# An encoder layer in three stages: its SBUF pools in another order, and two groups of loads on GpSimd's queue

## The chip, the cores and the metric

One core of one Trainium2 chip runs the whole kernel. The metric is the device time of one execution in microseconds (us). TensorE (PE) multiplies, VectorE (DVE), ScalarE (ACT) and GpSimd (POOL) do the rest, SyncE (SP) issues DMAs. Lines such as L42 or L1061 are lines of the kernel file.

## The reference

One encoder layer on a sequence of 2048 tokens of width 1024, all in float32:

```python
mod = silu(c) @ w_ada + b_ada                      # six vectors: shift, scale, gate, twice
h = rmsnorm(x, g_norm1) * (1 + sc1) + sh1
q_sb, k_sb, v_sb, q_ca, k_ca, v_ca = split(h @ w_in)     # 8 + 8 heads of 64
o_sb = stick_breaking_attention(q_sb, k_sb, v_sb)  # causal; weights from a running product
o_ca = chunked_relpos_attention(rms(q_ca), rms(k_ca), v_ca, rel_bias)  # own chunk + 8 before
x = x + gt1 * (concat(o_sb, o_ca) @ w_o)
h = rmsnorm(x, g_norm2) * (1 + sc2) + sh2
x = x + gt2 * (square(relu(h @ w1)) @ w2)          # 4096 wide in the middle
```

## The kernel before

Tokens are cut into four blocks of 512 (tb or g = 0 to 3, the latest first), width into eight slices of 128. A float32 product is made of three matmuls: each operand is split into a high part (ACT casts it, L128) and a low part (DVE or POOL subtracts, L129), and `mm3` multiplies high by high, high by low and low by high. What one stage hands to the next lies in DRAM scratch tensors: `scr_q`, `scr_k`, `scr_v`, `scr_w` (split weights), `scr_wo` (split w_o), `scr_m` (attention outputs), `scr_x` (the residual stream), `scr_h`, `scr_hid`, `scr_s`.

**Stage 1, projections.** Norm of x, the modulation vectors (`ada`), and the projections of most pieces of w_in. The last job is piece 5 for block 1. Tiles: `cb`, `cs` (pool adap), `wa` (adaw), `xt` (xp), the normed blocks `wide`, `ht2`, `ht0` (hp), the raw, high and low weights `wr`, `wh`, `wl` (wp), stores and turned heads (stp), norms (np_).

**Stage 2, attention.** A list of units (a head and a block of 512 queries, with 512 keys for the stick-breaking heads SB, or 1024 for the chunk heads CA), each of four steps. A step's order on PE, ACT, DVE and POOL is written out by hand (`Ordered` keeps each of these queues in the order of the program): transposes of weights made 8 steps ago (`wt`), scores of the next (`z`, `cz`), running product (`p`, a scan on DVE) or softmax, splits `wth`, `wtl`, value products (`acc`). POOL multiplies `b` by `p`, or scales `e`. Between the steps `fill` hands PE other matmuls as credit allows: the projections left over (`fill_qkv`: weights `fw`, banks `pf`) and the output projection of a finished block (`outproj(g)`, g = 3, 2, 1: weights `ow`, operand `mx`, banks `po`, residual `xr`). `outproj` loads `mo` (three buffers) and splits it slice by slice in `part(k)`; `part(k)` also starts the load of slice k + 3. What is left of the fillers runs after the last step (`drain`). Loads of q, k and v go through SP, those of the first two units through POOL's queue (`ldq`).

**Stage 3, MLP.** SP, ACT, DVE and POOL are not held to the order of the program here; the compiler's scheduler sets it from its own model, and PE keeps the program's. First the output projection of block 0: eight steps `Mixed(0, n)`, each 24 matmuls in one bank (`pso`). Step 0 loads the eight slices of `scr_m` (tile `m`, shown as `cm`) and splits them (`opm`); each step loads two halves of split weights (`wo`, four buffers) and a slice of x (`cxr`); `residual` (L209, DVE) adds, and SP stores to `scr_x` (L210). Then the first MLP product as seven sub-products of a Strassen-like scheme (`First`), whose right operands `h{i}_{k}` come from `right_blocks(mb, k)`, k = 0 to 3: four slices of `scr_x` loaded into temporaries `y` (pool tp, seven buffers, shown as `ty`), each multiplied by the row norm on POOL (L1062) and by scale and shift on ACT (L1063), then summed and split into seven `h` tiles. Then `Second`, the same for w2.

**Where tiles lie.** Pools of one stage are laid one behind the other in the order in which they are opened, and those of the next stage start again at the same place. The list `RESTS` sets how many steps a filler rests at each `yield` of a word ("pause" 3, "next" 1, "start" 10). In KB per partition, counted from the end of what lives through stages 1 and 2 (the 32 KB before that place, -32 to 0, hold pool hxp: the odd blocks `ht1`, `ht3`, later `mx`), worked out from the sizes of the tiles:

| stage | before |
|---|---|
| 1 | adap 0-8, adaw 8-24, xp 24-44, hp 44-76, wp 76-124, stp 124-156, np_ 156-167 |
| 2 | kp (q, k, v) 0-44, fp (`fw`/`ow`, `st`, `mo`, `xr`) 44-92, wtp (`wth`, `wtl`) 92-108, zp (`b`/`e`, `p`/`s`) 108-153, op (`o`, `otmp`, bias) 153-168 |
| 3 | hop (28 tiles `h`) -32-80, opp (split operands) 80-112, rawp (raw weights, `wo`) 112-128, accp (`cm`, `cxr`, kept sums) 128-152, tp 152-166, np2 from 166 |

Nothing in the source says what a tile waits for; the compiler derives the semaphores from which memory was used before.

Of the kernel before, what the change touches and what calls it, by code (L numbers as in the profile page):

```python
# [67 lines left out]
def encoder_kernel(ctx, tc, xT, c, g1, g2, w_in, gqk, bias, w_o, w1, w2, w_ada, b_ada, out):  # L68
# [151 lines left out]
    with ExitStack() as ph:  # L220
        adap = ph.enter_context(tc.tile_pool(name="adap", bufs=1))
        adaw = ph.enter_context(tc.tile_pool(name="adaw", bufs=4))
        xp = ph.enter_context(tc.tile_pool(name="xp", bufs=KT + 2))
        hp = ph.enter_context(tc.tile_pool(name="hp", bufs=1))
        wp = ph.enter_context(tc.tile_pool(name="wp", bufs=2))
        stp = ph.enter_context(tc.tile_pool(name="stp", bufs=4))
        np_ = ph.enter_context(tc.tile_pool(name="np_", bufs=2))
        pp = ph.enter_context(tc.tile_pool(name="ppA", bufs=8, space=PSUM))
# [298 lines left out]


    with ExitStack() as ph:
        kp = ph.enter_context(tc.tile_pool(name="kp", bufs=3))  # L530
        fp = ph.enter_context(tc.tile_pool(name="fp", bufs=3))
        wtp = ph.enter_context(tc.tile_pool(name="wtp", bufs=4))
        zp = ph.enter_context(tc.tile_pool(name="zp", bufs=2))
        op = ph.enter_context(tc.tile_pool(name="op", bufs=2))
        ppz = ph.enter_context(tc.tile_pool(name="ppz", bufs=4, space=PSUM))
        ppo = ph.enter_context(tc.tile_pool(name="ppo", bufs=2, space=PSUM))
# [226 lines left out]
        def fill_qkv(tb, ht, pieces):  # L763
# [12 lines left out]
            for n, piece in enumerate(pieces):  # L776
                grp, hf = divmod(piece, 2)
                w, nxt = nxt, []
                for j in range(2):
                    nm = f"f{tb}_{piece}_{j}"  # L780
                    ps = ppd.tile([P, TB], F32, tag="ps", name=f"p{nm}")
                    last = 0 if grp < 2 else 1
                    for tt in range(last + 1):
                        tl = slice((2 * j + tt) * P, (2 * j + tt + 1) * P)
                        for k in range(KT):
                            if n + 1 < len(pieces) and j and tt == last and k in (0, 4):
                                nxt.append(load(pieces[n + 1], k // 4))
                            wk = w[k // 4][:, k % 4]
                            for i, (a, b) in enumerate(((0, 0), (0, 1), (1, 0))):
                                flags = {"start": k == 0 and i == 0, "stop": k == KT - 1 and i == 2}  # L790
                                if grp < 2:
                                    pe.matmul(ps, wk[:, a, j * P : (j + 1) * P], ht[:, k, b, :], **flags)
                                    yield 1.0
                                else:
                                    pe.matmul(ps[:, tt * CW : (tt + 1) * CW], ht[:, k, b, tl], wk[:, a, :], **flags)
                                    yield 0.5

                    def keep():
                        if grp < 2:
                            store_qk(grp, 0, ps, fp, hf * 2 + j, tb, nm)  # L800
                        else:
                            store_v(grp // 3, ps, fp, hf, tb, j, nm)
                        if j:
                            have.add((piece, tb))

                    yield keep

        def outproj(g):
# [18 lines left out]
                fetch(k)  # L827
            nxt = load(0)
            yield "pause"
            part(0)  # L830
            yield "next"
            part(1)
            yield "next"
            for n in range(KT):
                w, xr = nxt
                if n + 1 < KT:
                    nxt = load(n + 1)
                ps = ppd.tile([P, TB], F32, tag="ps", name=f"po{g}_{n}")
                for k in range(KT):
                    if n == 0 and k + 2 < KT:  # L840
                        part(k + 2)
                    for i, (l, m) in enumerate(((0, 0), (0, 1), (1, 0))):
                        pe.matmul(
                            ps, w[:, l, k, :], mx[:, k, m, :], start=k == 0 and i == 0, stop=k == KT - 1 and i == 2
                        )
                        yield 1.0
# [154 lines left out]
    scr_hid = scratch("scr_hid", [P, 2, TB], 2, 8, NP // 2)  # L1001
    scr_s = scratch("scr_s", [P, 2, TB], 7, NP // 2)
    with ExitStack() as ph:
        hop = ph.enter_context(tc.tile_pool(name="hop", bufs=1))
        opp = ph.enter_context(tc.tile_pool(name="opp", bufs=8))
        rawp = ph.enter_context(tc.tile_pool(name="rawp", bufs=4))
        accp = ph.enter_context(tc.tile_pool(name="accp", bufs=12))
        tp = ph.enter_context(tc.tile_pool(name="tp", bufs=7))
        np2 = ph.enter_context(tc.tile_pool(name="np2", bufs=2))
        pp = ph.enter_context(tc.tile_pool(name="ppM", bufs=8, space=PSUM))  # L1010

# [45 lines left out]
        def right_blocks(mb, k):  # L1057
            y = {}
            for nm, tb, kk in (("11", 2 * mb + 1, k), ("12", 2 * mb, k), ("21", 2 * mb + 1, k + HK), ("22", 2 * mb, k + HK)):
                t = y[nm] = temp(f"y{mb}_{k}_{nm}")  # L1060
                sp.dma_start(t, scr_x[tb, kk])  # L1061
                pool.tensor_tensor(t, t, rows[tb], op=ALU.mult)  # L1062
                act.activation(t, t, AF.Identity, scale=aff[:, 1, kk : kk + 1], bias=mod[:, 3 * KT + kk : 3 * KT + kk + 1])  # L1063

            def put(i, src):
                hops[i, k] = hop.tile([P, 2, TB], F32R, tag=f"h{i}_{k}", name=f"h{mb}_{i}_{k}")
                operand(src, "", dst=hops[i, k])

# [187 lines left out]
        class Mixed(Step):  # L1256
# [9 lines left out]
            def prepare(self):  # L1266
                g, n = self.g, self.n
                if n == 0:
                    for k in range(KT):
                        m = kept(f"m{g}_{k}")  # L1270
                        sp.dma_start(m, scr_m[g, k])
                        Mixed.parts[k] = operand(m, f"m{g}_{k}", dve if k % 2 else pool)

            def load(self):
# [21 lines left out]

        steps += [Mixed(0, n) for n in range(KT)]
        for k in range(HK):
            at(2 + k, lambda k=k: right_blocks(1, k))
        for mb in (1, 0):  # L1300
            if mb:
                for j in range(NP):
# [64 lines left out]
```

## Time and profile before

| | us |
|---|---|
| median of 3 runs | 2782.63 (2777.75 to 2788.34) |
| the profiled execution | 2779.07 |
| its span, first to last instruction | 2777.3 |
| PE busy | 2644.2 (95%) |
| DVE, ACT, POOL busy | 1996.5, 1510.8, 1077.7 |
| stage 1, until the last projection matmul | about 494 |
| stage 2, until the last output projection matmul of its fillers | 494 to 1474 |
| stage 3 | 1474 to 2777 |

PE's busy time is the union of its matmuls, so its idle time is what the other 5% hold. In a row of the timeline stand start, duration, engine, line, operation, tile written and tiles read, how many instructions were merged, and in brackets the idle time of the engine before the row with what ended it. SPq and POOL rows of DMAs show the issue, not the transfer. The releaser in brackets is inferred from semaphores; where several were awaited, the last event stands there, and a DMA named there can be another one that shares its semaphore.

### The profile page before, as it was taken

Reading aid. Unit: us, or ns where it says so; the run is one execution under the profiler, and the core shown is the slowest. Engines: PE = TensorE matmul, PEld = TensorE weight load, DVE = VectorE, ACT = ScalarE, POOL = GpSimd, SP = SyncE. Lnnn points to the kernel's source line nnn. Section 1 sums busy time; section 2 is a strip of 40 time slices with the busy share of each in tenths; the row PEclk is TensorE's granted clock in tenths of the full one; section 3 lists DMA queues with packets and bytes.
Section 4 is the critical chain, followed back from the end, with each engine's and each line's share of the span. In section 5 each row is a group of like instructions: output and inputs, shape, how many; then the busy total and the mean of one; then the engine's idle time right before and its main releaser. Section 6 shows DMA issues by size and latency. Waiting matters only on the chain. (4 is left out here: it accounts for less than half of the span.)

```text
span 2777.3 us, 43035 instructions
## 1 busy us (share of the span) xinstructions
PE 2644.2 (95%) x14192; PEld 2244.7 (81%) x14192; DVE 1996.5 (72%) x3365; ACT 1510.8 (54%) x2884; POOL 1077.7 (39%) x1126
## 2 busy tenths in 40 slices
PE   5899989889999999989997999999999999999999
PEld 4699989678888997868786788888878888888887
DVE  8467576679789887979775887876587666655564
ACT  2322332678678878878763454455455445444443
POOL 5334364456546656777734433200021433300000
PEclk9899989899999999999998999999999999999999
DMA  7788975788887578655567777786567444465574
GB/s 249 252 302 291 347 244 207 237 243 244 268 262 234 193 210 261 195 169 185 169 206 263 252 275 260 268 291 239 188 243 266 152 148 167 152 208 191 196 257 171
DMA packets 309919, 635.71 MB, mean 229 GB/s; under 512 B 29248, under 2 KB 118336, under 8 KB 300608
## 3 DMA queue, kind: packets, MB, share of 16 engines
q1 hardware_dynamic: 309184, 631.39, 68.0%
q8 instruction: 112, 1.84, 0.3%
q0 software_dynamic: 512, 1.57, 0.2%
q14 instruction: 111, 0.91, 0.1%
HBM read 449.87 MB, written 182.98 MB: 228 GB/s over the span
## 5 line engine op out<-in xcount | busy, mean ns | idle before, releaser
L42 PE MATMUL ps<-oph,opv 128*128 128x512 f32 x2688 | 614.3, 390 | 3.7 <-DVE oph L129 2.0
L42 PE MATMUL ps<-h,opw 128*128 128x512 f32 x2688 | 610.2, 389 | 1.4 <-DVE cx L1019 1.1
L42 PEld LDWEIGHTS ps<-oph,opv 128*128 128x128 f32 x2688 | 505.1, 188 | 110.9 <-DVE oph L129 3.0
L42 PEld LDWEIGHTS ps<-h,opw 128*128 128x128 f32 x2688 | 504.3, 188 | 107.0 <-DVE cx L1019 1.5
L42 POOL TENSOR_TENSOR b<-b,p 128x512 f32<-128x512 f32 (+1 forms) x320 | 360.1, 1125 | 193.4 <-DVE p L42 174.3
L42 DVE TENSOR_TENSOR wtl<-wt,wth 128x512 fp32r<-128x512 f32 (+3 forms) x544 | 290.5, 545 | 50.4 <-ACT wth L42 47.5
L42 ACT CAST wth<-wt 128x512 fp32r<-128x512 f32 (+3 forms) x544 | 257.9, 484 | 117.0 <-PE wt L42 99.6
L42 PE MATMUL pt<-wh,ht 128*128 128x256 f32 x1664 | 311.1, 288 | 5.5 <-DVE ht L182 5.5
L129 DVE TENSOR_TENSOR oph<-hr,oph 128x512 fp32r<-128x512 f32 x224 | 155.6, 694 | 188.5 <-ACT oph L128 188.4
L128 ACT CAST oph<-hr 128x512 fp32r<-128x512 f32 x224 | 139.2, 622 | 276.1 <-PE ps L42 258.5
L42 PEld LDWEIGHTS pt<-wh,ht 128*128 128x128 f32 x1664 | 265.9, 195 | 6.8 <-DVE ht L182 6.7
L42 DVE TENSOR_TENSOR_SCAN p<-z,p,zero 128x512 f32<-128x512 f32 x192 | 245.9, 1281 | 35.2 <-ACT z L42 31.3
L42 PE MATMUL pt<-wl,ht 128*128 128x256 f32 x832 | 238.2, 286 | 0.0
L42 PE MATMUL acc<-wth,v 128*128 128x512 f32 (+3 forms) x544 | 221.7, 411 | 1.3 <-DMA v<-scr_v 1.3
L42 ACT ACTIVATE b<-z 128x512 f32<-128x512 f32 (+1 forms) x320 | 171.5, 536 | 68.0 <-PE z L42 40.6
L42 PE MATMUL z<-k,q 128*128 128x512 f32 (+3 forms) x640 | 188.9, 378 | 15.4 <-DVE p L42 11.4
L42 POOL TENSOR_TENSOR e<-e,cols 128x640 f32<-128x640 f32 (+4 forms) x128 | 143.5, 1123 | 147.9 <-DVE cols L42 110.9
L1019 POOL TENSOR_TENSOR ts<-w 128x512 f32<-128x512 f32 x32 | 45.3, 1415 | 363.8 <-DMA w<-in_w_dram 234.9
L42 PE MATMUL acc<-wtl,v 128*128 128x512 f32 (+3 forms) x544 | 186.2, 349 | 0.0
L42 PE MATMUL po<-mx,ow 128*128 128x512 f32 x576 | 164.9, 401 | 11.7 <-POOL mx L42 7.5
L42 PE MATMUL wt<-ident,b 128*128 128x128 f32 x1088 | 173.2, 275 | 1.8 <-DVE p L42 0.7
L42 ACT ACTIVATE z<-z 128x512 f32<-128x512 f32 (+1 forms) x320 | 170.1, 532 | 0.0
(211 smaller groups left out, 4760.3 us busy)
## 6 DMA issues: line engine op xcount, KB each, us to landing
hr<-scr_hid SPq DMA_DIRECT2D x112, 512.0 KB, 3.3
v<-scr_v SPq DMA_DIRECT2D x136, 256.0 KB, 3.7
k<-scr_k SPq DMA_DIRECT2D x268, 128.0 KB, 4.1
w<-in_w_dram SPq DMA_DIRECT2D x64, 512.0 KB, 4.1
wr<-scr_s SPq DMA_DIRECT2D x64, 512.0 KB, 4.2
q<-scr_q SPq DMA_DIRECT2D x124, 256.0 KB, 4.9
fw<-scr_w SPq DMA_DIRECT2D x28, 1024.0 KB, 7.0
wa<-in_w_ada_dram SPq DMA_DIRECT2D x48, 512.0 KB, 6.4
```

Of the source, the lines that this page charges most:

```text
L42: return lambda *x, **y: self.tc.keep_in_program_order(f(*x, **y))
L128: act.copy(hi, src)
L129: (lo_eng or dve).tensor_tensor(lo, src, hi.bitcast(F32), op=ALU.subtract)
L1019: eng.tensor_tensor(out, a, b, op=op)
```

## The change

Four things, none of which changes what is computed or how many instructions of a kind run:

- The pools are opened in another order, one (`st` of stage 2, now pool fsp) is taken out of fp, and hop is cut in three: hop1 holds the seven `h` tiles of k = 1 and one of k = 2, hop0 those of k = 0, hop2 the other thirteen.
- `outproj` does four `part`s at a step each before its first matmul, where it did two, and the last four between the first row's matmuls, where it did six.
- The eight loads of `m` and the sixteen loads of `y` for mb = 1 (blocks 3 and 2) are issued by POOL, where SP issued them.
- `right_blocks(1, k)` is called at steps 0, 2, 4, 6, where it was called at 2, 3, 4, 5.

| stage | after |
|---|---|
| 1 | adap 0-8, adaw 8-24, xp 24-44, wp 44-92, hp 92-124, stp 124-156, np_ 156-167 |
| 2 | zp 0-45, kp 45-89, fp 89-125, fsp 125-137, wtp 137-153, op 153-168 |
| 3 | hop1 -32-0, opp 0-32, rawp 32-48, accp 48-72, tp 72-86, hop2 86-138, hop0 138-166, np2 from 166 |

```diff
@@ -221,8 +221,8 @@
         adap = ph.enter_context(tc.tile_pool(name="adap", bufs=1))
         adaw = ph.enter_context(tc.tile_pool(name="adaw", bufs=4))
         xp = ph.enter_context(tc.tile_pool(name="xp", bufs=KT + 2))
+        wp = ph.enter_context(tc.tile_pool(name="wp", bufs=2))
         hp = ph.enter_context(tc.tile_pool(name="hp", bufs=1))
-        wp = ph.enter_context(tc.tile_pool(name="wp", bufs=2))
         stp = ph.enter_context(tc.tile_pool(name="stp", bufs=4))
         np_ = ph.enter_context(tc.tile_pool(name="np_", bufs=2))
         pp = ph.enter_context(tc.tile_pool(name="ppA", bufs=8, space=PSUM))
@@ -527,10 +527,11 @@
 
 
     with ExitStack() as ph:
+        zp = ph.enter_context(tc.tile_pool(name="zp", bufs=2))
         kp = ph.enter_context(tc.tile_pool(name="kp", bufs=3))
         fp = ph.enter_context(tc.tile_pool(name="fp", bufs=3))
+        fsp = ph.enter_context(tc.tile_pool(name="fsp", bufs=3))
         wtp = ph.enter_context(tc.tile_pool(name="wtp", bufs=4))
-        zp = ph.enter_context(tc.tile_pool(name="zp", bufs=2))
         op = ph.enter_context(tc.tile_pool(name="op", bufs=2))
         ppz = ph.enter_context(tc.tile_pool(name="ppz", bufs=4, space=PSUM))
         ppo = ph.enter_context(tc.tile_pool(name="ppo", bufs=2, space=PSUM))
@@ -797,9 +798,9 @@
 
                     def keep():
                         if grp < 2:
-                            store_qk(grp, 0, ps, fp, hf * 2 + j, tb, nm)
+                            store_qk(grp, 0, ps, fsp, hf * 2 + j, tb, nm)
                         else:
-                            store_v(grp // 3, ps, fp, hf, tb, j, nm)
+                            store_v(grp // 3, ps, fsp, hf, tb, j, nm)
                         if j:
                             have.add((piece, tb))
 
@@ -827,18 +828,17 @@
                 fetch(k)
             nxt = load(0)
             yield "pause"
-            part(0)
-            yield "next"
-            part(1)
-            yield "next"
+            for k in range(4):
+                part(k)
+                yield "next"
             for n in range(KT):
                 w, xr = nxt
                 if n + 1 < KT:
                     nxt = load(n + 1)
                 ps = ppd.tile([P, TB], F32, tag="ps", name=f"po{g}_{n}")
                 for k in range(KT):
-                    if n == 0 and k + 2 < KT:
-                        part(k + 2)
+                    if n == 0 and k + 4 < KT:
+                        part(k + 4)
                     for i, (l, m) in enumerate(((0, 0), (0, 1), (1, 0))):
                         pe.matmul(
                             ps, w[:, l, k, :], mx[:, k, m, :], start=k == 0 and i == 0, stop=k == KT - 1 and i == 2
@@ -1001,11 +1001,13 @@
     scr_hid = scratch("scr_hid", [P, 2, TB], 2, 8, NP // 2)
     scr_s = scratch("scr_s", [P, 2, TB], 7, NP // 2)
     with ExitStack() as ph:
-        hop = ph.enter_context(tc.tile_pool(name="hop", bufs=1))
+        hop1 = ph.enter_context(tc.tile_pool(name="hop1", bufs=1))
         opp = ph.enter_context(tc.tile_pool(name="opp", bufs=8))
         rawp = ph.enter_context(tc.tile_pool(name="rawp", bufs=4))
         accp = ph.enter_context(tc.tile_pool(name="accp", bufs=12))
         tp = ph.enter_context(tc.tile_pool(name="tp", bufs=7))
+        hop2 = ph.enter_context(tc.tile_pool(name="hop2", bufs=1))
+        hop0 = ph.enter_context(tc.tile_pool(name="hop0", bufs=1))
         np2 = ph.enter_context(tc.tile_pool(name="np2", bufs=2))
         pp = ph.enter_context(tc.tile_pool(name="ppM", bufs=8, space=PSUM))
 
@@ -1058,11 +1060,12 @@
             y = {}
             for nm, tb, kk in (("11", 2 * mb + 1, k), ("12", 2 * mb, k), ("21", 2 * mb + 1, k + HK), ("22", 2 * mb, k + HK)):
                 t = y[nm] = temp(f"y{mb}_{k}_{nm}")
-                sp.dma_start(t, scr_x[tb, kk])
+                (pool if mb else sp).dma_start(t, scr_x[tb, kk])
                 pool.tensor_tensor(t, t, rows[tb], op=ALU.mult)
                 act.activation(t, t, AF.Identity, scale=aff[:, 1, kk : kk + 1], bias=mod[:, 3 * KT + kk : 3 * KT + kk + 1])
 
             def put(i, src):
+                hop = hop0 if k == 0 else hop1 if k == 1 or (k, i) == (2, 1) else hop2
                 hops[i, k] = hop.tile([P, 2, TB], F32R, tag=f"h{i}_{k}", name=f"h{mb}_{i}_{k}")
                 operand(src, "", dst=hops[i, k])
 
@@ -1268,7 +1271,7 @@
                 if n == 0:
                     for k in range(KT):
                         m = kept(f"m{g}_{k}")
-                        sp.dma_start(m, scr_m[g, k])
+                        pool.dma_start(m, scr_m[g, k])
                         Mixed.parts[k] = operand(m, f"m{g}_{k}", dve if k % 2 else pool)
 
             def load(self):
@@ -1296,7 +1299,7 @@
 
         steps += [Mixed(0, n) for n in range(KT)]
         for k in range(HK):
-            at(2 + k, lambda k=k: right_blocks(1, k))
+            at(2 * k, lambda k=k: right_blocks(1, k))
         for mb in (1, 0):
             if mb:
                 for j in range(NP):
```

## The prediction

> **What bounds the kernel now.** I read the page, then PE's own list of waits, then the timeline of every engine where those waits lie.
>
> ```profile
> span 2777.3 us, 43035 instructions
> PE 2644.2 (95%) x14192; PEld 2244.7 (81%) x14192; DVE 1996.5 (72%) x3365; ACT 1510.8 (54%) x2884; POOL 1077.7 (39%) x1126
> PE z L42 <- DVE p L42: 11.4, 11, 6.6
> PE pso L42 <- DMA wo<-scr_wo: 7.7, 4, 4.8
> PE po L42 <- POOL mx L42: 7.5, 3, 5.1
> PE pso L42 <- DMA cxr<-in_xT_dram: 7.3, 1, 7.3
> PE po L42 <- ACT mx L42: 4.2, 1, 4.2
> ```
>
> PE is idle 2777.3 - 2644.2 = 133 us of the span. The rows of waits (total, times, longest) name what this change can reach: `pso`, 15 us, is the start of stage 3; `po`, 11.7 us, the output projections inside attention; the one wait of 6.6 us on `p` is the start of attention. No matmul is removed, so the change can give back only idle time, and the slow matmuls behind it.
>
> **From attention to the MLP (the main term).** PE's timeline, then one stretch of windows each for the waits and for steady running (PEclk, the granted clock, is third from the end):
>
> ```profile
> 1452.30 22.02 PE L42 MATMUL po<-mx,ow 128*128 128x512 f32 x96
> 1481.64 0.79 PE L42 MATMUL pso<-opm,wo 128*128 128x512 f32 x1 [7.32 <-DMA cxr<-in_xT_dram]
> 1501.86 14.02 PE L42 MATMUL pso<-opm,wo 128*128 128x512 f32 x48 [4.78 <-DMA wo<-scr_wo]
> 1517.00 5.75 PE L42 MATMUL pso<-opm,wo 128*128 128x512 f32 x24 [1.12 <-DMA wo<-scr_wo]
> 1541.30 3.35 PE L42 MATMUL ps<-h,opw 128*128 128x512 f32 x14
> 1502.00:1517.00 15.00, 13.88 (x48) 10.84 (x48) 12.26 (x18) 6.59 (x10) 6.58 (x3) 0.80 0.75 250
> 1517.00:1541.30 24.30, 22.39 (x95) 17.52 (x95) 18.47 (x26) 12.65 (x20) 10.71 (x7) 1.00 0.83 280
> ```
>
> From 1452.30 to 1474.32 PE does nothing but drain the fillers, 96 matmuls of 22.02 / 96 = 0.229 us. The 192 matmuls of `Mixed` then take from 1474.32 to 1541.30, 67.0 us, where 192 x 0.229 = 44.0 would do; behind the wait of 4.78 us the granted clock is 0.80 over 15 us, so a wait costs more than its length. Why the first waits:
>
> ```profile
> 1480.97 4.26 ACT L128 CAST opm<-cm 128x512 fp32r<-128x512 f32 x8 [27.89 <-DMA cxr<-in_xT_dram]
> 1475.14 0.32 SPq L210 DMA_DIRECT2D scr_x<-xr  x1
> scr_x<-xr SPq DMA_DIRECT2D x24, 256.0 KB, 4.6
> 1453.84 0.32 SPq L578 DMA_DIRECT2D scr_m<-o  x1
> DMA to landing us min/median/max: 6.8/6.8/6.8
> L42 POOL TENSOR_TENSOR mx<-mo,mx x8: 1277/1286/1297, 1361.0 to 1381.4; 128x512 fp32r<-128x512 f32 x8
> 1450.28 0.49 PE L42 MATMUL wt<-ident,e 128*128 128x128 f32 x3
> 1452.19 0.27 PE L42 MATMUL acc<-wtl,v 128*128 128x128 f32 x1
> ```
>
> The row of landings belongs to the one `scr_m` store above it.
>
> All eight casts start together at 1480.97, 5.8 us after the store of the last `xr` was issued. The first `opm` buffer lies on `mo`, not on `xr`, and `mo` was last read by the `mx` split that starts at 1381.4: the wait is for the pool fp as a whole. In the new layout opp lies on zp, whose last reader (a transpose of `e`) ends at 1450.8, rawp on zp and kp, accp and tp on kp, whose last reader (a value product) ends at 1452.5. So `cm`, four `wo`, `cxr` and seven `y` can be loaded and split under the 22 us of drain; only `cm`'s last slice waits for the store issued at 1453.84. It lands at 1460.7, so the load behind it has 13.6 us until 1474.3 and another 21 x 0.229 = 4.8 until slice 7 is used. The 24 loads are 24 x 0.62 us (below) = 15 us of POOL's time, and POOL is idle there. The two first rows of `Mixed` then run at 24 x 0.229 = 5.5 us; the other six reload `wo` behind the row two before, at the pace that rows 4 to 7 show now, (1541.30 - 1517.00) / 4 = 6.1. Sum 2 x 5.5 + 6 x 6.1 = 47.6, against 67.0: 19.4 us. I take 18, since the loads are now bunched beside the last `ow`. Bounds: 67.0 - 44.0 = 23.0 above, and 7.3 below (the first wait alone).
>
> What would be late next is `h`: `First` needs all four k.
>
> ```profile
> L129 DVE TENSOR_TENSOR h<-ty,h x28: 678/685/1786, 1494.8 to 1539.3; 128x512 fp32r<-128x512 f32 x28
> 1489.66 7.98 POOL L1062 TENSOR_TENSOR ty<-ty,r 128x512 f32<-128x512 f32 x6
> ```
>
> 28 tiles in 44.5 us now end 2 us before PE needs them, no slack. After: hop0 lies on wtp and op, free when the last `scr_m` store has landed (1460.7), so k = 0 goes under the drain; hop1 is hxp, free at 1474.3; hop2 holds fp and still waits until about 1481. Then three blocks remain, each 7 splits and 4 sums x 0.685 = 7.5 us of DVE: about 1504, before `Mixed` ends at 1522. The calls at 4 and 6 in place of 4 and 5 stay inside that.
>
> **From projections to attention.** The end of stage 1 on PE, SP and ACT, with POOL's present loads and the groups of DMAs (the last number is us from issue to landing):
>
> ```profile
> 494.26 1.04 PE L42 MATMUL px<-ident,qh 128*128 128x128 f32 x8
> 494.49 0.33 SPq L771 DMA_DIRECT2D fw<-scr_w  x1
> 504.45 0.60 ACT L42 ACTIVATE b<-z 128x512 f32<-128x512 f32 x1 [8.24 <-DMA scr_k<-st]
> 506.85 1.22 PE L42 MATMUL z<-k,q 128*128 128x512 f32 x2 [6.64 <-DVE p L42]
> 396.12 1.24 POOL L545 DMA_DIRECT2D q<-scr_q  x2 [5.47 <-issue]
> q<-scr_q POOLq DMA_DIRECT2D x4, 256.0 KB, 12.4
> 510.21 1.08 SPq L545 DMA_DIRECT2D q<-scr_q  x2
> q<-scr_q SPq DMA_DIRECT2D x124, 256.0 KB, 4.9
> fw<-scr_w SPq DMA_DIRECT2D x28, 1024.0 KB, 7.0
> 516.25 1.86 PE L42 MATMUL pf<-ht,fw 128*128 128x512 f32 x7
> ```
>
> Now `b` waits until 504.45 for the stores of `st`, since zp lies on stp. After, zp lies on adap, adaw, xp and 1 KB of wp, all free at 494.3: that wait goes. But kp, whose first tiles were loaded at 396, now lies wholly on wp, and `fw` shows how that ends: its first buffer lies on hp alone, yet it was issued at 494.49, right behind the last projection matmul, when wp fell free. So `q` and `k` of the first two units go from 396 to 494.3. Four issues of 0.62 us, then the landing: 4.9 us by the row of SP's queue, 12.4 by POOL's, whose four loads at 396 ran beside the store of a whole normed block (`scr_h`). `z` would then start at 494.3 + 2.5 + 4.9 = 501.7 or at 509.2, `b` 1.2 us later (the two matmuls of the row at 506.85), at 502.9 or 510.4: -1.5 to +6 us against 504.45. `st`'s last stores, `v` and the next units' loads run beside them; I take 0. `fw` now waits for stp (about 504) and is first used at 516.25, with 7.0 us to land: hidden, at an exposure of 2 us.
>
> By the Trainium skill (DMA: Bandwidth & Descriptors, "Anatomy of one DMA") a load on GpSimd's path takes about 2.0 us and its bytes at 436 GB/s, as an estimate 2.6 us for 256 KB; the POOL row shows 12.4, so the trace does not agree under load. By it `b` would start at 494.3 + 2.5 + 2.6 + 1.2 = 500.6 and this term would be -4 us.
>
> **The output projections in attention.**
>
> ```profile
> 1214.08 1.38 PE L42 MATMUL po<-mx,ow 128*128 128x512 f32 x3 [1.74 <-POOL mx L42]
> 1220.58 0.80 PE L42 MATMUL po<-mx,ow 128*128 128x512 f32 x1 [5.13 <-POOL mx L42]
> 1215.03 0.16 DVE L42 TENSOR_TENSOR ntm<-nym 128x4 f32<-128x4 f32 x1 [4.93 <-POOL nym L42]
> 1218.04 1.26 POOL L42 TENSOR_TENSOR b<-b,p 128x512 f32<-128x512 f32 x1 [2.90 <-DVE p L42]
> 1201.23 0.74 PE L42 MATMUL z<-k,q 128*128 128x512 f32 x2 [0.65 <-DVE p L42]
> ```
>
> PE waits for `mx` here, but in the same steps DVE waits 4.9 us for `nym` of the norm of the block before, which POOL reaches late behind `b` and `mx`; `b` follows at 1218.04, and PE's next transposes need it until 1219.3. Two more steps before the first `po` let PE step past `mx`, not past `b`: of 1.74 + 5.13 I expect 2 to 3 us here, 1 to 2 of the 4.2 on ACT's `mx` for g = 1, nothing for g = 3. Against it, 2 steps more for three projections run without filler, at an idle of 0.65 each: 6 x 0.65 = 3.9, of which some is idle now. Bounds: -11.7 (all of `po`'s waits) and +3.9. I take -2.5.
>
> **Sum.** -18 + 0 - 2.5 = -20.5 on the profiled 2779.07 us (span 2777.3 and 1.8 around it): 2758.6. The median of the three runs is 3.6 above that execution, so the forecast for the median is 2782.6 - 20.5 = 2762. About 0.5%, 13.9 us, is what a measurement of this kernel can tell from no change.
>
> **Rivals.**
>
> *Only the first wait goes.* `Mixed` keeps its later pace because DVE's and SP's queues still hold `residual` and the next `wo` behind `h`: 7.3 us and 2.0 of the 2.5 stay, so 2773. For it: PE waited until 1501.86 because SP issued `wo` only here, behind a `scr_x` store that waited for DVE:
>
> ```profile
> 1497.60 0.38 SPq L1278 DMA_DIRECT2D wo<-scr_wo  x1
> ```
>
> Against it: with `y` off SP's queue and k = 0 done early, less stands ahead.
>
> *The layout costs at the start of attention what it would save.* The rule of whole pools makes kp wait for the last matmul, and POOL's landing is as at 396: +6, and +2 for `fw` behind it: 2770.
>
> *Slower: the chain of `y` becomes serial on POOL.* POOL's queue is in order. If each block's four loads find no free `y` until the block before is split, a block costs a landing of 12.4, 4 x 1.33 of POOL and 7.5 of DVE, 25.2 us; four from 1460.7 end at 1561.5, and `First` starts 22 us later than 1541.3: 2782.6 + 22 - 2.5 = 2802. It decides above (1539.3 - 1460.7) / 4 = 19.7 us a block. Against it: seven `y` buffers let half of the next block load ahead. The Trainium skill (SBUF — State Buffer, "SBUF: two separate sides") speaks for this rival: GpSimd cannot write descriptors while DVE holds the shared port, and a DMA of 620 ns became about 3100. The POOL row above shows 0.62 us an issue; by the rule the eight loads of k = 2 and 3, which fall beside DVE's work, cost an estimated 20 us more of POOL's time, which makes the chain longer and is no term of the sum.
>
> **How the numbers follow.** Forecast 0.58, first rival 0.23, second 0.10, slower 0.09. The range is 2748 (23.0 at the boundary, the whole 11.7 at `po`) to 2780; the slower case and a part of the first rival lie outside. Faster by over 0.5% (below 2768.7): the forecast and 0.02 of the second, 0.60. Within: 0.31. Slower: 0.09.
>
> **What would show it.** Right: the first `pso` follows the last `po` without a gap over 1 us; `Mixed` takes 46 to 50 us; POOL's `cm` and first `y` loads lie between 1452 and 1465; `fw` is issued behind the landing of `st`; `q` and `k` of unit 0 are issued at about 494. Wrong: casts of `opm` that wait for an `xr` store, `ps` waiting for `h`, POOL idle behind a `y` load for over 10 us, or `z` of the first unit after 510.

## The result, and the profile after

The changed kernel takes 2800.2 us (median of 5, 2796.0 to 2801.1) where the kernel before, beside it, takes 2787.0 (2777.8 to 2791.9): the ratio is 1.0050, with a 95% interval of 1.0029 to 1.0072. It is slower by 0.5%; the forecast of 2762 and its range are missed, and the sign is wrong. The profiled executions are 2800.98 (span 2799.2) after and 2779.07 before.

PE's list of waits in the changed kernel (in all, times, longest):

```profile
PE z L42 <- DVE p L42: 14.4, 17, 6.0
...
PE wt L42 <- DVE cols L42: 10.2, 5, 4.8
PE z L42 <- issue: 8.9, 1, 8.9
PE pso L42 <- ACT h L128: 8.4, 1, 8.4
PE pso L42 <- DMA wo<-scr_wo: 7.7, 4, 3.4
...
PE po L42 <- DVE xr L42: 4.6, 1, 4.6
```

Three rows that the change aimed at are gone: `po` on POOL's and on ACT's `mx`, `pso` on `cxr`; the fourth, `pso` on `wo`, is 7.7 us as before. Others stand in their place: `z` on `p` (11.4 before) and `wt` on `cols` (4.7 before) in attention, `po` on `xr` at the end of the drain, and `pso` on `h`, 8.4 us where `cxr` was 7.3. So where did the time arise? PE runs the same matmuls in both kernels, so the start of one matmul in each trace, subtracted, tells how late a kernel is at that point. The table does that for the profiled executions of the changed kernel and of runs that are told of below (us against the kernel before; the first column is its own time; matmuls are counted from 0):

| matmul | before | changed | e1 | e3 | e5 | e9 | e10 | e12 |
|---|---|---|---|---|---|---|---|---|
| `z` no. 300 of 640 | 915.1 | +6.4 | +3.0 | -3.5 | +1.1 | +0.2 | +0.7 | -6.9 |
| last `acc` | 1452.2 | +13.7 | +10.4 | +4.0 | +8.5 | +8.0 | +1.0 | -6.8 |
| first `pso` | 1481.6 | +22.6 | +5.7 | +3.8 | +3.5 | +3.1 | -3.9 | -6.8 |
| first `ps` of the MLP | 1541.3 | +19.8 | +11.8 | +4.1 | +13.1 | +0.8 | -7.4 | -11.4 |
| its 300th | 1611.4 | +22.8 | +16.7 | +4.2 | +15.0 | +6.0 | -2.2 | -6.3 |
| last matmul | 2772.7 | +21.9 | +15.8 | +4.2 | +13.8 | +6.5 | -3.3 | -7.5 |

The changed kernel loses about 6 us before `z` no. 300, 7 more from there to the last value product, where the output projections lie, and 9 between it and the first `pso`; `Mixed` gives 3 back and the first products of the MLP take 3 again. From the last `acc` to the first `ps` it thus takes 94.9 us where the kernel before takes 88.8: +6.1 at the boundary, where the forecast said -18; at the start of attention it said 0. A column is one execution, and those of one kernel differ by several us: the profiled one of the kernel before lies 8 us under its median, so the 21.9 of the last row is more than the 13.2 between the medians.

**The boundary.** First DVE and SP in the kernel before, then PE, DVE and POOL after:

```profile
1474.36 0.75 DVE L42 SCALAR_TENSOR_TENSOR xr<-po,mod,xr 128x512 f32<-128x512 f32 x1 [4.69 <-DMA wo<-scr_wo]
1482.19 6.36 DVE L129 TENSOR_TENSOR opm<-cm,opm 128x512 fp32r<-128x512 f32 x4 [7.09 <-ACT opm L128]
...
1450.83 0.81 SPq L1271 DMA_DIRECT2D cm<-scr_m  x2
```

```profile
1466.01 16.58 PE L42 MATMUL po<-mx,ow 128*128 128x512 f32 x72
1487.21 8.58 PE L42 MATMUL po<-mx,ow 128*128 128x512 f32 x24 [4.62 <-DVE xr L42]
1504.23 14.41 PE L42 MATMUL pso<-opm,wo 128*128 128x512 f32 x50 [8.45 <-ACT h L128]
1522.04 5.73 PE L42 MATMUL pso<-opm,wo 128*128 128x512 f32 x24 [3.40 <-DMA wo<-scr_wo]
...
1561.12 1.07 PE L42 MATMUL ps<-h,opw 128*128 128x512 f32 x4
```

```profile
1474.22 0.83 DVE L129 TENSOR_TENSOR opm<-cm,opm 128x512 fp32r<-128x512 f32 x1 [5.92 <-ACT opm L128]
1474.98 0.74 DVE L42 SCALAR_TENSOR_TENSOR xr<-po,mod,xr 128x512 f32<-128x512 f32 x1
...
1485.80 0.69 DVE L129 TENSOR_TENSOR opm<-cm,opm 128x512 fp32r<-128x512 f32 x1 [5.31 <-ACT opm L128]
1486.41 0.75 DVE L42 SCALAR_TENSOR_TENSOR xr<-po,mod,xr 128x512 f32<-128x512 f32 x1
1489.15 2.70 DVE L129 TENSOR_TENSOR h<-ty,h 128x512 fp32r<-128x512 f32 x1 [2.00 <-ACT h L128]
...
1496.17 0.75 DVE L42 SCALAR_TENSOR_TENSOR xr<-po,mod,xr 128x512 f32<-128x512 f32 x1
...
1503.38 0.75 DVE L42 SCALAR_TENSOR_TENSOR xr<-po,mod,xr 128x512 f32<-128x512 f32 x1
```

```profile
1466.48 2.81 POOL L1274 DMA_DIRECT2D cm<-scr_m  x5 [11.42 <-PE acc L42]
...
1474.46 0.57 POOL L1274 DMA_DIRECT2D cm<-scr_m  x1
...
1476.32 1.11 POOL L1274 DMA_DIRECT2D cm<-scr_m  x2
```

Before, DVE does all residuals `xr` of the drain first, the last at 1474.36, right behind its `po`, and the splits `opm` after it. Now read DVE's rows after from top to bottom: its queue is in order, and in it the splits of stage 3 stand ahead of each of the drain's last four residuals `xr`. The first split waits 5.92 us for a `cm`, the one at 1485.80 waits 5.31 us for the last `cm`, which POOL issued in the row at 1476.32, behind two of its own splits. The residual at 1486.41 frees a bank of `po`: PE's last row stood 4.62 us for it and then took 8.58 us, where 24 matmuls take 5.5. The last residual, whose `po` was done at 1495.8, stands behind six more instructions of stage 3 and the residual of the row before until 1503.38, and 0.1 us after its end comes the first `pso`. The bracket names ACT's `h`, the last event before; that `pso` awaits the residual is inferred from the program, where its pool of banks lies over those of stage 2, and in e1, e5 and e10 too the first `pso` comes 0.1 us behind that residual. So pools did fall free early and loads did start under the drain, and with them stage 3's work came to stand ahead of work on which PE hangs.

**The start of attention after** (POOL, SP, PE and ACT):

```profile
494.00 1.24 POOL L546 DMA_DIRECT2D q<-scr_q  x2 [9.68 <-issue]
...
506.42 0.81 SPq L772 DMA_DIRECT2D fw<-scr_w  x2
...
503.15 1.19 PE L42 MATMUL z<-k,q 128*128 128x512 f32 x2 [8.86 <-issue]
...
504.56 0.60 ACT L42 ACTIVATE b<-z 128x512 f32<-128x512 f32 x1 [9.35 <-PE z L42]
```

Here all is about as forecast: the loads of q and k at 494.0, `fw` late but hidden, the first `b` at 504.56 where it was 504.45. The 6 us of the table arise later. At `z` no. 48, at about 537 us, the changed kernel is still 0.8 us ahead; by no. 64, at 609, behind the first chunk heads, it is 6.0 behind.

### The profile page after: what moved, and what is told of

Its sections match the earlier page's. It is cut to its first block, busy times and chain, and to the rows that moved or that the text cites. A ratio compares the mean times of both kernels' runs of the same rounds, so it can differ in the third digit from the quotient of the medians.

```text
span 2799.2 us, 43036 instructions
## 1 busy us (share of the span) xinstructions
PE 2651.8 (95%) x14192; PEld 2251.8 (80%) x14192; DVE 2007.2 (72%) x3365; ACT 1510.3 (54%) x2884; POOL 1082.7 (39%) x1150
## 4 chain that ended last, share of the span: by engine, by line
PE 73%; DVE 8%; DMA 6%; issue 6%; ACT 3%; POOL 3%; SPq 1%; DVEq 0%; ACTq 0%; POOLq 0%
PE ps L42 42%; PE acc L42 5%; PE wt L42 5%; PE pt L42 5%; PE pf L42 5%; PE z L42 5%; PE po L42 3%; DMA k<-scr_k 1%; PE cz L42 1%; DVE cb L42 1%; DMA ty<-scr_x 1%; DVE p L42 1%; POOL cy L133 1%; PE pq L42 1%; ACT e L42 1%
```

## The experiments

Each ran in 5 rounds beside the kernel before, whose median was 2783.0 to 2783.9 in these jobs. Ratios are to it.

**Are the drain's residuals the loss at the boundary? (e1)** DVE's splits of stage 3 are held behind them:

```diff
-Mixed.parts[k] = operand(m, f"m{g}_{k}", dve if k % 2 else pool)
+Mixed.parts[k] = operand(m, f"m{g}_{k}", Ordered(tc, dve) if k % 2 else pool)
 ... # and in right_blocks, where mb: every split and column_sum by Ordered(tc, dve)
```

> The changed kernel with one thing added: DVE's subtractions of `opm` and of the first blocks' `h` are held to the order of the program, so they stand behind the last four residuals `xr` of the drain on DVE's queue. Theory 1 (the drain's residuals stand on DVE behind stage 3's splits, which wait for `cm` and `y`; PE's last row waits for their bank and `pso` for the release of all of stage 2's banks): the wait of 4.62 us before the last 24 `po` goes, these run in about 5.5 us where they took 8.6, and of the 8.45 us before the first `pso` about 7 go: 4.6 + 3.1 + 7 = 15 us, so about 2786. Theory 2 (the last `cm` lands late, at 1485, beside the last `ow`, and `opm` is what is late): PE's drain gets faster but the first `pso` stays near 1500, at most 4 us come back: 2796 or more.

Measured: 2794.5 us, ratio 1.0045 (1.0029 to 1.0061), between the two theories. PE's timeline, and one stretch of windows:

```profile
1480.71 5.72 PE L42 MATMUL po<-mx,ow 128*128 128x512 f32 x24 [1.39 <-DMA ow<-scr_wo]
1487.32 17.08 PE L42 MATMUL pso<-opm,wo 128*128 128x512 f32 x72 [0.89 <-issue]
1507.99 1.22 PE L42 MATMUL pso<-opm,wo 128*128 128x512 f32 x2 [3.59 <-DMA wo<-scr_wo]
```

```profile
1475.00:1486.40 11.40, 10.01 (x44) 7.66 (x42) 0.75 (x1) 4.11 (x6) 6.74 (x9) 1.00 1.03 416
```

Both waits went as theory 1 says: the last row takes 5.72 us, and `pso` follows after 0.89. By the table the first `pso` comes 17 us sooner than in the changed kernel. But `Mixed` grew from 57 to 66 us, with four waits of 3.5 to 4.2 us for `wo`: much of the gain is given back later.

**What does the edit of `outproj` cost? (e2, e3)** e2 takes it out of the changed kernel, e3 puts it alone into the kernel before. In e2 (the other way round in e3):

```diff
-for k in range(4):
+for k in range(2):          # two parts ahead of the first row
     part(k)
     yield "next"
 ...
-if n == 0 and k + 4 < KT:
-    part(k + 4)
+if n == 0 and k + 2 < KT:
+    part(k + 2)
```

> The changed kernel with `outproj` as it was (two parts ahead, six between the matmuls of the first row). If the edit of `outproj` is what moved the end of the last value product from +6 us (at 1040) to +13.7 us (at 1466), this one ends 6 to 8 us earlier, at about 2793, and the waits on POOL's `mx` are back. If the prediction's -2.5 us for this edit was right and the drift has another cause (the layout, the order of loads), it ends at about 2802.

Measured: 2789.7, ratio 1.0029 (1.0016 to 1.0042), against 1.0050 with it; the waits of `po` on `mx` are back, at 11.6 us.

> The kernel before with only the edit of `outproj` (four parts ahead). If the edit costs by itself: 2787 + 6 to 8 = about 2794, the z waits of 6.0 and 4.9 us at the start of the projections for blocks 2 and 1 are there, and the waits on POOL's `mx` are gone. If the prediction's -2.5 us was right: 2784.5.

Measured: 2789.1, ratio 1.0024 (1.0014 to 1.0035). The edit alone costs 0.24%, 6.7 us. ACT, PE and a stretch of windows of e3 at the start of the first projection:

```profile
1064.96 0.62 ACT L42 CAST mx<-mo 128x512 fp32r<-128x512 f32 x1 [4.34 <-DMA mo<-scr_m]
...
1066.12 0.33 PE L42 MATMUL wt<-ident,e 128*128 128x128 f32 x1 [2.69 <-DVE wtl L42]
```

```profile
1068.00:1083.00 15.00, 14.34 (x74) 12.12 (x74) 9.86 (x35) 8.94 (x23) 7.39 (x7) 0.80 0.62 187
```

The first fill after the rests issues seven `po` at once, and with them three `part`s. The third casts a slice whose load was issued one step before, since three buffers hold `mo`. ACT waits 4.34 us for it in order, with the next `wth` behind it, DVE's `wtl` behind that, and PE 2.69 us; then the granted clock is 0.80 over 15 us.

**Is it that wait? (e7)** e3, with `mo` loaded straight into the low half of `mx`, all eight slices at once:

```diff
-mo[k] = fp.tile([P, TB], F32, tag="xs", name=f"mo{g}_{k}", bufs=3)
+mo[k] = mx[:, k, 1, :].bitcast(F32)
 ...
-if k + 3 < KT:
-    fetch(k + 3)
-for k in range(3):
+for k in range(KT):
     fetch(k)
```

> The kernel before with four parts ahead, and with `mo` loaded straight into the low half of the operand `mx`, all eight slices at the start of the projection, where it went through three buffers that `part` refills. Theory 1 (the edit of `outproj` costs 6.7 us by itself because three casts of `mx` come in one step and ACT waits in order for the slice whose load was issued one step before: ACT's idle before `mx` is 11.3 us with four parts, 7.9 with two): ACT's waits for `mo` are nearly gone and the cost falls to 2 us or less, 2785 or below. Theory 2 (the cost is the two more steps a projection without filler): it stays at 5 to 7 us, about 2789.

Measured: 2780.9, ratio 0.9993 (0.9983 to 1.0003). The whole cost is gone, as theory 1 has it. ACT's idle time before `mx` (in all, times) is 11.0 us in the changed kernel and 7.9 in the kernel before; in e7 no such row is left.

```profile
  DMA mo<-scr_m: 11.0, 5
```

Could `mo` in the operand be a gain of its own that hides the cost? The traces say no. The kernel before takes 537.1 us from `z` no. 300 to the last `acc`. The seven traces with four parts and three buffers (the changed kernel, e1, e3, e4, e5, e6, e9) take 7.3 to 7.9 us more. The two with four parts and `mo` in the operand (e7, e11) take 0.3 to 0.4 less. The four others with two parts lie between 0.4 less and 0.3 more, with `mo` in the operand (e8, e10, e12) or without (e2). So the wait for `mo` is the cost, and without it four parts gain next to nothing over two.

**What does stage 3's part cost? (e4)** The changed kernel with stage 3 as it was:

```diff
-hop1, hop2, hop0             # three pools
+hop = ph.enter_context(tc.tile_pool(name="hop", bufs=1))
-(pool if mb else sp).dma_start(t, scr_x[tb, kk])
+sp.dma_start(t, scr_x[tb, kk])
-pool.dma_start(m, scr_m[g, k])
+sp.dma_start(m, scr_m[g, k])
-at(2 * k, lambda k=k: right_blocks(1, k))
+at(2 + k, lambda k=k: right_blocks(1, k))
```

> The changed kernel with stage 3 as before: one pool hop, `m` and `y` loaded by SP, right_blocks at steps 2 to 5. Stages 1 and 2 keep the new order of pools and the four parts. If stage 3's part of the change costs 6 us from the last value product to the first product of the MLP and about 2 behind it, as the two profiles say, this one ends at about 2792, and the start of attention and the projections keep their +13.7. If the +6 between 540 and 600 was an accident of one execution, it ends at about 2787.

Measured: 2791.9, ratio 1.0042 (1.0027 to 1.0058): the number that was expected, though the interval does not part it from the changed kernel, and its trace does not bear the expectation out. From the last `acc` to the first `ps` it takes 93.0 us, 1.9 less than the changed kernel and not 6. What stage 3 of before does restore is DVE's order: each residual of the drain stands right behind its `po`, and PE's 96 last `po` run without a wait in 22.0 us; the first `pso` then waits 9.78 us, by the bracket for `wo`. With the 6.7 us of the parts taken off, about 5 are left for the new pools of stages 1 and 2, with an uncertainty as large; some of it lies at the boundary (93.0 us against 88.8).

**Why does `Mixed` slow down once the drain is free? (e5, e6)** e5 holds only the `opm` (as in e1) and the first three `h`:

```diff
-operand(src, "", dst=hops[i, k])
+held = mb and k == 0 and i in (1, 2, 3)
+operand(src, "", Ordered(tc, dve) if held else None, hops[i, k])
```

> The changed kernel with only those subtractions of DVE held to the order of the program that stood ahead of the drain's residuals: the four of `opm` and the first three of `h` of k = 0. The other `h` keep the scheduler's order, which the run with all of them in the program's order lost: there a block took 15.7 us and `h` ended at 1555, where it was 12.6 us and 1539.5 in the changed kernel. Theory 1 (the residuals behind stage 3's splits cost the boundary, and that run gave the gain back by the order of `h`): first `pso` within 1.5 us of the last `po`, `h` done by about 1537, row 0's residual within 5 us of its last matmul; 12 to 17 us less than the changed kernel: 2784 to 2788. Theory 2 (the first rows of `Mixed` wait for `wo` because DMA is full: 410 GB/s and a share of 1.0 from 1475 to 1486): `Mixed` stays at 60 us or more and the time at about 2794.

Measured: 2792.1, ratio 1.0036 (1.0023 to 1.0050); neither theory as written. PE, DVE and SP of e5:

```profile
1485.15 11.62 PE L42 MATMUL pso<-opm,wo 128*128 128x512 f32 x50 [0.89 <-issue]
...
1508.52 1.22 PE L42 MATMUL pso<-opm,wo 128*128 128x512 f32 x2 [6.27 <-DMA wo<-scr_wo]
...
1497.21 0.69 DVE L129 TENSOR_TENSOR h<-ty,h 128x512 fp32r<-128x512 f32 x1 [5.70 <-ACT h L128]
...
1502.04 0.74 DVE L209 SCALAR_TENSOR_TENSOR cxr<-pso,mod,cxr 128x512 f32<-128x512 f32 x1
...
1502.81 0.32 SPq L210 DMA_DIRECT2D scr_x<-cxr  x1
1503.22 0.38 SPq L1282 DMA_DIRECT2D wo<-scr_wo  x1
```

Row 0 of `Mixed` ends at about 1490.7, when SP issues the `wo` of row 2, but its residual comes at 1502.04, behind `h`, which waits for `y`. SP's queue holds row 0's store and behind it a `wo`, issued at 1503.22, that PE has needed since 1502. DMA is not full up to there: from 1490.7 to 1503.0 its share is 0.38, at 152 GB/s. This is the forecast's first rival, in a kernel whose first wait is gone.

e6 is e5 with the loads of `wo` and the stores of `Mixed` kept in program order on SP (osp), a row's store behind later loads:

```diff
-sp.dma_start(w[l].bitcast(F32), scr_wo[n,][:, l, :, :])
+(osp if n > 1 else sp).dma_start(w[l].bitcast(F32), scr_wo[n,][:, l, :, :])
 ...                          # behind the loads of a row:
+self.store(2)                # osp stores held rows until two are left
 ...                          # in run, where the store was issued:
+Mixed.held.append((g, n, xr))
```

> The run with the seven subtractions held, and the stores of `Mixed`'s rows held back on SP until the `wo` of two rows later have been issued. Theory 1 (SP's queue: the next `wo` stands behind a store that waits for DVE's residual): the waits for `wo` after the third row go, `Mixed` takes 46 to 52 us, another 4 to 8 us less: about 2780. Theory 2 (the landing of `wo`, 5.4 us for 512 KB and two of them a row, sets the pace): no change against the run without it.

Measured: 2793.6, ratio 1.0035 (1.0021 to 1.0049), no change, and yet not theory 2: e5's four waits of 2.7 to 6.3 us became one of 19.2.

```profile
1543.25 9.03 PE L42 MATMUL pso<-opm,wo 128*128 128x512 f32 x24 [19.15 <-DMA wo<-scr_wo]
...
1537.43 0.75 DVE L1295 SCALAR_TENSOR_TENSOR cxr<-pso,mod,cxr 128x512 f32<-128x512 f32 x1
...
1519.63 18.89 SPq L42 DMA_DIRECT2D scr_x<-cxr  x2
1538.63 0.87 SPq L42 DMA_DIRECT2D wo<-scr_wo  x2
```

SP issued the second of two stores ahead of the last `wo`, and stood at it until DVE's fifth residual was done at 1538.2; which row's store it is, the trace does not tell. Order on SP alone does not help while DVE hands the residuals over late.

**DVE's order set by hand (e9).** Rows and blocks alternate: the residual of row 0, `h` of k = 0, row 1, k = 1, and so on; the `opm` are held as in e1.

```diff
+residual(g, n, ps, xr, Ordered(tc, dve))          # in Mixed.run
+operand(src, "", Ordered(tc, dve) if mb and i in (1, 2, 3) else None, hops[i, k])
-at(2 * k, lambda k=k: right_blocks(1, k))
+at(1 + k, lambda k=k: right_blocks(1, k))
```

> The changed kernel with DVE's order set by hand where the boundary hangs on it: drain's residuals, `opm`, row 0's residual, `h` of k = 0, row 1's residual, `h` of k = 1 and so on (right_blocks called at steps 1 to 4). Theory 1 (after the drain's wait is gone, `Mixed` waits for `wo`, whose load stands on SP behind the store of a row two before, whose residual stands on DVE behind `h` that waits for `y`; in the run with seven subtractions held, row 0 ended at 1490 and its residual came at 1502): `Mixed` takes 47 to 53 us, the first product of the MLP starts 75 to 82 us after the last value product (94.9 in the changed kernel, 88.8 before), 2778 to 2784. Theory 2 (the chain of `y` on POOL decides, 12 to 16 us a block): `Mixed` is fast, but the first product waits for the last `h` until 88 us or more after the last value product: 2790.

Measured: 2787.1, ratio 1.0015 (1.0005 to 1.0025), about 10 us below the changed kernel. From the end of the last `acc` to the first product of the MLP it takes 81.6 us, as theory 1 says, where the changed kernel takes 94.9 and the one before 88.8. `Mixed` takes 55.8, above theory 1's 47 to 53, with waits of 4.6 and 1.5 us for `wo` left. After two of the first products PE then waits 4.5 us for `opw`, which neither theory names, and the time is 3 us above theory 1. That wait ends 87 us behind the last `acc`, near the 88 of theory 2; what stands ahead of `opw` is shown with e10.

**All together, first without that order (e8), then with it (e10).** e8 is e6, and e10 is e9, each with the diffs of e2 (two parts) and e7 (`mo` in the operand).

> Everything that the theories ask for: the changed kernel's pools and queues, the seven subtractions held, the stores held back on SP, `outproj` with two parts ahead again and `mo` loaded into the operand. If each loss is where the theories put it: 2800 less 15 for the residuals, 5 for `wo`, 6 for the parts and up to 6 for ACT's waits for `mo`: 2768 to 2775, below the kernel before. If the layout itself costs 5 us or more at the start of attention and in the first product of the MLP, as the run with the old stage 3 hints: 2776 to 2782.

Measured: 2783.9, ratio 1.0007 (0.9997 to 1.0018), above both sums: e6's single wait for `wo` is in it, 17.9 us.

> The run with DVE's order set, and `outproj` with two parts ahead again and `mo` loaded straight into the operand. If theory 1 of that run holds, and the cost of `outproj`'s edit is ACT's wait for `mo`: 6 to 10 us below it, 2770 to 2776, faster than the kernel before by about 0.3%. If the boundary's gain goes to the chain of `y`: about 2782.

Measured: 2777.7, ratio 0.9979 (0.9969 to 0.9989), faster than the kernel before by 0.2%, between the two expectations. The timelines of PE, ACT and DVE:

```profile
1477.71 3.92 PE L42 MATMUL pso<-opm,wo 128*128 128x512 f32 x16 [0.89 <-issue]
...
1507.28 14.24 PE L42 MATMUL pso<-opm,wo 128*128 128x512 f32 x50 [5.44 <-DMA wo<-scr_wo]
...
1533.88 0.73 PE L42 MATMUL ps<-h,opw 128*128 128x512 f32 x2 [1.46 <-ACT opw L128]
1540.14 20.03 PE L42 MATMUL ps<-h,opw 128*128 128x512 f32 x81 [5.52 <-DVE opw L129]
...
1533.22 0.61 ACT L128 CAST opw<-w 128x512 fp32r<-128x512 f32 x1
...
1533.34 1.72 DVE L129 TENSOR_TENSOR h<-ty,h 128x512 fp32r<-128x512 f32 x1 [0.68 <-ACT h L128]
...
1538.32 1.75 DVE L129 TENSOR_TENSOR opw<-w,opw 128x512 fp32r<-128x512 f32 x1
```

The boundary's last wait is of the same kind as the first. ACT has cast `opw` at 1533.8, but its subtraction stands on DVE behind work on `h` of k = 3 and comes at 1538.32, and PE waits for it 5.52 us. The same wait is 4.5 us in e9 and e12 and 4.4 in e11.

**Are the new pools worth anything then? (e11)** The kernel before, its pools and its `cm` on SP kept, with the diffs of e7 and e9, four parts and the loads of `y` on POOL:

```diff
-at(2 + k, lambda k=k: right_blocks(1, k))
+at(1 + k, lambda k=k: right_blocks(1, k))
-sp.dma_start(t, scr_x[tb, kk])
+(pool if mb else sp).dma_start(t, scr_x[tb, kk])
```

> The pools of before, with the rest of what the runs point to: DVE's order set by hand at the boundary, `y` loaded by POOL, four parts ahead and `mo` loaded into the operand. It differs from the run before it in this job by the layout (and by four parts instead of two, which cost nothing once `mo` does not wait). If the layout is what lets stage 3 begin under the drain: the first `pso` stays about 7 us behind the last `po`, `y` is loaded 8 us later, and the time is 5 to 8 us more than with the new pools, less the 4 us or so that the new pools seem to cost at the start of attention: 2772 to 2780. If the layout brings nothing at the boundary: it is the faster by those 4 us.

Measured: 2783.0, ratio 1.0001 (0.9989 to 1.0013), above both expectations. With the pools of before the first `pso` waits, as e11's timeline of PE shows:

```profile
1481.95 0.79 PE L42 MATMUL pso<-opm,wo 128*128 128x512 f32 x1 [9.81 <-ACT opm L128]
```

So with the order set, e10 is 0.2% faster than e11, and the boundary is where, by these two traces: at the last `acc` e10 stands 3.2 us behind e11, at the first `pso` 4.2 ahead. The two differ in the number of parts and in the queue of `cm` too, so that the gain is that of the pools together with their loads.

**The start of attention (e12).** In e10, kp is opened ahead of zp:

```diff
-zp = ph.enter_context(tc.tile_pool(name="zp", bufs=2))
 kp = ph.enter_context(tc.tile_pool(name="kp", bufs=3))
+zp = ph.enter_context(tc.tile_pool(name="zp", bufs=2))
```

> The fastest run so far (DVE's order set at the boundary, two parts, `mo` into the operand) with kp opened ahead of zp in stage 2: kp then lies on adap, adaw and xp, as in the kernel before, and zp on wp, where the changed kernel has the two the other way round. Theory 1 (the new layout gains nothing at the start of attention only because it moves the loads of q and k from 396 to 494): the loads are back at about 396, `b` no longer waits for the stores of `st`, the first `z` comes at about 497 and the first `b` at 498 where it was 504 to 505; 4 to 7 us less: 2771 to 2774. Theory 2 (what follows, up to 600, is paced by the chain of unit after unit and by the loads of the chunk heads): the first `b` comes 6 us earlier and the time stays within 2 us of 2778.

Measured: 2770.4 us (2767.4 to 2774.5), ratio 0.9953 (0.9940 to 0.9967): theory 1. POOL's loads are back at 398 (first and last start in the row), and PE and ACT begin 5 us sooner than in the changed kernel:

```profile
L546 POOL DMA_DIRECT2D q<-scr_q x4: 517/550/722, 398.6 to 408.2; - x4
```

```profile
498.55 0.73 PE L42 MATMUL z<-k,q 128*128 128x512 f32 x2 [1.84 <-DVE st L196]
...
499.44 0.60 ACT L42 ACTIVATE b<-z 128x512 f32<-128x512 f32 x1 [1.82 <-PE z L42]
```

This version beats both kernels, by 0.5% and 1.0%.

## Why the prediction was wrong, step by step

**Boundary, -18.** This step failed: from the last `acc` to the first `ps` the change costs 6.1 us. The change did open the pools: `cm` was issued from 1466.5 on, 0.3 us behind the last `acc`, two `wo` at 1468.8 and the first `y` at 1478.7. What failed is "loaded and split under the 22 us of drain": it put the splits of stage 3 at nothing, and did not ask where they stand in DVE's order against the drain's four residuals. The runs showed waits of 4.62 and 8.45 us of PE for these residuals, and both went when the splits were held behind them (e1, e5). The front matter says that stage 3's order is the scheduler's own, so the question was there. The loads hung on the same order: the other two `wo` and `cxr` came only from 1487.6 on, behind a store on SP that needed the residual of 1486.41. Two smaller faults: in the kernel before, SP already issued `cm` from 1450.83 on and all four `wo` by 1472.4, so the casts of `opm` were what waited, and these 12 of the 24 loads had nothing to gain; and POOL's issues cost 0.55 to 0.64 us each, about as taken, but stand in one queue with POOL's splits, so that the last `cm` was issued at 1476.9, 10.4 us behind the first. The pace of 47.6 us for `Mixed` was not reached in any run; 57.0 in the changed kernel and 54.7 (e10) at best, since a residual still passes DVE behind `h`: in e10 that of row 1, at 1498.17, ahead of the store and the `wo` for which PE waits 5.44 us. "About 1504" for the last `h` failed too: a block costs 12.6 us, not 7.5, since `y`, its scaling and the turns between ACT and DVE stand in it. It did not decide, with 21 us to spare.

**Start of attention, 0.** The mechanism is right, and its numbers within 2.5 us; that gain and cost cancel to 0.1 us at `b` is luck within the -1.5 to +6 that it worked out. It missed what lies behind: at `z` no. 300, the nine traces with the new pools in stages 1 and 2 (the changed kernel's among them, e12's not) are at +2.4 us on average (-2.0 to +7.0), the four with the old pools (that of before among them, at 0) at -2.5 (-4.5 to 0). About 2 of these 5 us arise between `z` no. 48 and no. 64; no run shows their cause, and the changed kernel's trace, with 6.8 us there, is the worst of the nine (the others -0.6 to 4.5). And e12 shows that the term was a choice, not a price: against e10, 7 us were to be had by the order of two lines.

**Output projections, -2.5.** Wrong in sign and outside its bounds (-11.7 to +3.9), at +6.7. "Let PE step past `mx`, not past `b`" was right: the wait of 5.13 us on `mx` came back as one of 6.0 on `p` (5.82 in e7, which loses nothing). What failed is the count against it, two steps of 0.65 us idle: the price is not in the steps that run without filler but in the burst of three `part`s behind them, with three buffers for `mo`, and in what follows PE's wait.

**Rivals.** The first ("only the first wait goes") named the mechanism that e5 shows, but as gain not made; it becomes a loss where the first wait is replaced. The second's mechanism did not show at `b`, which came at 504.56 and not at 510.4. The third gave 2802, near the result, by luck: the chain of `y` takes 12.6 us a block, under the 19.7 from which it decides. The Trainium skill (SBUF — State Buffer, "SBUF: two separate sides") had been put beside it, with a DMA of 620 ns that became about 3100 beside a DVE `tensor_copy`. DVE's work here is subtractions of two inputs, and the trace shows no such slowing of POOL's issues (min, median and longest in ns), several of which lie beside them:

```profile
L1063 POOL DMA_DIRECT2D ty<-scr_x x16: 546/587/589, 1478.7 to 1526.7; - x16
```

**Signs named beforehand.** Two signs of being right failed: the first `pso` came 8.45 us behind the last `po`, and `Mixed` took 57 us. `fw` behind `st`, and q and k at 494, came as named. None of the four signs of being wrong appeared (`z` came at 503, before 510), though the forecast was wrong: that the boundary could fail by a residual that stands too late was not among them.

## What to carry to other kernels

A pool that falls free earlier lets the next stage's work start earlier, and also lets it stand in an in-order queue ahead of what still has to finish: before counting the gain, list for each engine what the stage before still has to issue, and fix that order by hand. A chain of such queues (a residual on DVE, its store and the next load on SP) is mended where the late hand-over is, not further down: e6 moved the wait, e9 took most of it away. Where a job is put off to issue it in a burst, count the buffers that it is fed from.

## What the runs showed of the hardware

Matmuls behind a wait of PE can run at a lower granted clock, but do not behind every wait. In the changed kernel, behind 4.62 us of waiting, 24 matmuls took 8.58 us at a granted clock of 0.65; in e1, behind 1.39 us, the same 24 took 5.72 at 1.00. In e3, 2.69 us of waiting stand ahead of 15 us at 0.80. But behind a wait of 3.40 us in the changed kernel 24 matmuls took 5.73 us at 1.00, and the 48 behind the next wait, of 2.24 us, took 12.79 at 0.87.

A subtraction on DVE has a median of 686 ns, but up to 2697 in this row of the changed kernel:

```profile
L129 DVE TENSOR_TENSOR h<-ty,h x28: 678/686/2697, 1489.2 to 1539.5; 128x512 fp32r<-128x512 f32 x28
```

The long ones of `h` and `ty` lie beside POOL's multiplications of `ty`, 1.3 us each in the median. The Trainium skill (SBUF — State Buffer, "SBUF: two separate sides") says that DVE and GpSimd share a port pair as an exclusive lock, also for a DVE instruction with two inputs in SBUF against a GpSimd one that reads SBUF; these rows agree.

The transfers of both queues together, mostly loads of 256 KB and 512 KB, reached 416 GB/s at a share of 1.0 (e1, 1475 to 1486), near the 436 that the same section of the Trainium skill gives as the peak. In the changed kernel the loads of `cm` took 4.7 us to land at the least, 6.5 in the median and 8.2 at the most.

Open: what the new pools cost between `z` no. 48 and no. 64, in the first chunk heads, and why; and which part of stage 3's edit (pools, queues or steps) made the scheduler put the splits ahead of the residuals.
